# A hybrid decoder layer on one core: conv rows in place, 26 taps in the two-way filter, high parts ahead of low parts, two rows kept for the layer norm

## The chip, the cores and the metric

The kernel runs on one core of a Trainium2 chip. Its time is the device time of one execution in microseconds (us). Three runs of the kernel before took 827.59, 824.11 and 824.79 us, median 824.79 us. A profile is one execution recorded by the hardware profiler. The engines are PE (matmul), PEld (its weight load), DVE (vector), ACT (activation), POOL (GpSimd) and SP (it issues DMAs). POOL issues DMAs too, among them those that add to what lies at their destination.

## What is computed

One layer of a decoder with two mixers, on 1024 prompt positions and 8 sample positions, 1032 columns in all, in fp32:

```python
h = _rmsnorm(x, norm_g)
z = h @ w_in                                        # 1024 -> 6144
a_val, a_gl, a_gate, b_u, b_v, b_gate = split(z)    # 1024 each
a_in = a_val * sigmoid(a_gl)
a_conv = depthwise_conv(concat(conv_buf, a_in), conv_w) + conv_b   # 31 taps
a_out = silu(layernorm(a_conv, a_ln_g, a_ln_b)) * silu(a_gate)
vn = layernorm(b_v, b_ln_g, b_ln_b)
b_out = b_u * spatial_gate(vn, w_s, b_s) * silu(b_gate)
y = x + concat(a_out, b_out) @ w_out                # 2048 -> 1024
y = _rmsnorm(y, final_g)
```

The conv states and the last chunk of `b_v` are outputs as well. The layer norm of the conv branch runs over the 1024 channels, which lie on the partitions of eight tiles, the "rows" k = 0 to 7: its sums over channels are matmuls with a matrix of ones, and they need all eight rows.

## The kernel before

**In-projection.** There are 24 units of two output tiles each: P0 to P7 (values and gates for conv row k), v, B and G (the gMLP's values, its gated part, and the gates of the conv branch). Each step multiplies one unit by both halves of the columns with a seven-product scheme in the manner of Strassen (`PRODS`); the seven products are its "slots". Each fp32 operand is split into a high and a low part, and three passes (high by high, high by low, low by high) make one product, so that a slot has 48 matmuls into PSUM banks za, zb, zc and ze. The weights R of a unit are loaded by SP, summed on DVE (`wsum`, L153), their high parts H made on ACT (`whigh`, L164) and their low parts L on DVE (`wlow`, L168), which needs H. ACT moves partial products between banks (L973, L977, L981); `evac0` (L312, ACT) and `evac1` (L316, DVE) bring results out of PSUM into `row` and `apad`.

**Conv.** For each P unit, 31 taps run over the 1024 prompt positions of row k. Most go through a two-way filter: `d` holds differences of neighbours (L363), and for each pair of taps three DVE operations of 512 elements (L379) add to three tiles m[0], m[1] and m[2], of which the sums m[0]+m[1] and m[0]+m[2] are the even and the odd positions. The taps that are left are products on ACT (`prod`, L389 and L391), added up by POOL's accumulating DMAs (L395). `fin` writes c(k) from m with a step of two elements (L414) and adds the products to it, by a POOL DMA (for k = 7 by DVE). `acc_item` adds c(k) to `ssum` and writes it to DRAM (cD), both by POOL DMAs.

**Layer norm.** The mean's matmuls are lnm and lnms (L437, L440). Each c(k), reloaded from cD as `lc` except for k = 7, is centred (L454, `cen`) and squared on ACT. The squares are summed on DVE, and rows 0 to 3 go back to DRAM. lnv (L480) gives the variance, lnb (L503) spreads its inverse root to `lnr`. Then for each k: DVE multiplies by `lnr` (L523), ACT applies silu, DVE multiplies by the gate (L529), and `prep_m` makes the high part mh on ACT (L695) and the low part ml on DVE (L696). That chain of eight rows is called the chain below.

**Out-projection.** Its first half (steps s = 0 to 7, tiles pz and pzc, 72 matmuls a step) needs only the gMLP branch; its second half (po, three groups of columns by eight tiles) needs the conv branch. pz alternates between banks a and b, pzc is in bank c, and the first po tile goes to bank b, which pz7 held. `evac_h` (L718, L721) and `evac_o` (L726 to L732) add them to yt. After each group `stat_o`, `bcast_o` and `norm_o` make the last rms norm.

**What sets the order.** All large SBUF tiles share one pool of 51 places (tag "u", `NU`): a new tile takes the place that came free, and waits until the engines and DMAs that used it are done. Conv and layer norm work stands in a queue `fill`; `pump` takes from it whenever the estimated DVE time `est["dve"]` is behind the estimated PE time. The costs beside each entry are those estimates. An entry of kind "pe" is taken only from slot 3 on, and behind `delay`s. A larger estimate for DVE moves later entries to later slots.

Of the kernel before, what the change touches and what calls it, by code (L numbers as in the profile page):

```python
# [12 lines left out]
ALU = mybir.AluOpType  # L13
# [12 lines left out]
CW = 31  # L26
H = CW - 1
EPS = 1e-6
NF = 12
NU = 51  # L30
MMT = 0.12
KEEP_C = (4, 5, 6, 7)
KEEP_G = (6, 7)


# [7 lines left out]
def body(ctx, tc, xT, w_in, w_out, state, stateT, conv_w, vecs, wsT, w00, b_s,  # L43
# [7 lines left out]
    def U(shape, name, dt=F32):  # L51
        return pool.tile(shape, dt, tag="u", name=name, bufs=NU)
# [118 lines left out]
    def wsplit(u, i):  # L171
        whigh(u, i)
        wlow(u, i)
# [46 lines left out]
    def warm(n):  # L220
        p = PS("e", f"warm{slotno[0]}_{n}")
        for _ in range(n):
            T.matmul(p[:, 0, :128], lhsT=ones_m, rhs=ident, start=True, stop=True)
# [108 lines left out]
    cc = {}  # L332
    lnc = {}

    def acc_item(k):
        def acc():
            c = cc.pop(k)
            if k == 7:
                V.tensor_tensor(out=Ssum[0], in0=Ssum[0], in1=c, op=ALU.add)
                lnc[7] = c  # L340
                return
            if k == 0:
                Ssum[0] = U([128, NT], "ssum")
                G.dma_start(Ssum[0], c)
            else:
                G.dma_start(Ssum[0], c, accum_op=ALU.add)
            G.dma_start(cD[k], c)
        fill.append(("dve", 1.15 if k == 7 else 0.0, acc))

    def conv_items(k, ap):  # L350

        st = {}
        HN = NP_ // 2
        others = [0] + list(range(2 * NF + 1, CW))

        def start():
            d = U([128, 2, HN + NF - 1], f"d{k}")
            st["d"] = d  # L360
            n = 2 * (HN + NF - 1)
            for e in range(2):
                V.tensor_tensor(out=d[:, e, :], in0=ap[:, 1 + 2 * e:1 + 2 * e + n:2], in1=ap[:, 2:2 + n:2],  # L363
                                op=ALU.subtract)
            mm_ = U([128, 2, HN], f"m01_{k}")
            st["m"] = [mm_[:, 0, :], mm_[:, 1, :], U([128, HN], f"m2_{k}")]
            for e in range(3):
                A.activation(st["m"][e], src(e, 0), AF.Copy, scale=wt(e, 0))
        fill.append(("dve", 1.25, start))

        def src(e, i):
            return ap[:, 2 + 2 * i:2 + 2 * i + NP_:2] if e == 0 else st["d"][:, e - 1, i:i + HN]

        def wt(e, i):
            return cws[:, k, i:i + 1] if e == 0 else cw[:, k, 2 * i + e:2 * i + e + 1]

        def taps(i, e):
            def f():
                V.scalar_tensor_tensor(out=st["m"][e], in0=src(e, i), scalar=wt(e, i), in1=st["m"][e],  # L379
                                       op0=ALU.mult, op1=ALU.add)  # L380
            return f

        def gtap(n):

            def f():
                j = others[n]
                p = U([128, NP_], f"prod{k}_{j}")
                if n == 0:
                    A.activation(p, ap[:, j:j + NP_], AF.Identity, scale=cw[:, k, j:j + 1], bias=vec[:, CB, k:k + 1])  # L389
                else:  # L390
                    A.activation(p, ap[:, j:j + NP_], AF.Copy, scale=cw[:, k, j:j + 1])  # L391
                if n == 0:
                    st["g"] = p
                else:
                    G.dma_start(st["g"], p, accum_op=ALU.add)  # L395
            return f
        n = 0
        for i in range(1, NF):
            while n < len(others) and n * (NF - 3) < i * len(others):
                fill.append(("dve", 0.0, gtap(n)))  # L400
                n += 1
            for e in range(3):
                fill.append(("dve", 0.665, taps(i, e)))
            if i == 4 and k:
                acc_item(k - 1)

        def fin():
            c = U([128, NT], f"c{k}")
            cc[k] = c
            m = st.pop("m")  # L410
            V.scalar_tensor_tensor(out=c[:, NP_:], in0=ap[:, H + NP_:H + NT], scalar=cw[:, k, H:CW],
                                   in1=csmp[:, k, :], op0=ALU.mult, op1=ALU.add)
            for e in range(2):
                V.tensor_tensor(out=c[:, e:NP_:2], in0=m[0], in1=m[1 + e], op=ALU.add)  # L414
            g = st.pop("g")
            if k < 7:
                G.dma_start(c[:, :NP_], g, accum_op=ALU.add)
            else:
                V.tensor_tensor(out=c[:, :NP_], in0=c[:, :NP_], in1=g, op=ALU.add)
        fill.append(("dve", 1.4 if k < 7 else 2.6, fin))  # L420


    ln = {}
    mixa = {}

    def ln_items():
        acc_item(7)

        def lnload(k):
            lnc[k] = U([128, NT], f"lc{k}")  # L430
            SP.dma_start(lnc[k], cD[k])

        def mean():
            ln["m"] = U([128, NT], "lnmean")
            p = PS("e", "lnm")
            for q in range(2):
                T.matmul(p[:, q, :], lhsT=ones_m, rhs=Ssum[0][:, 512 * q:512 * q + 512], start=True, stop=True)  # L437
            A.activation(ln["m"][:, :NP_].rearrange("p (a b) -> p a b", a=2), p, AF.Copy)
            p = PS("e", "lnms")
            T.matmul(p[:, 0, :NS], lhsT=ones_m, rhs=Ssum[0][:, NP_:], start=True, stop=True)  # L440
            A.activation(ln["m"][:, NP_:], p[:, 0, :NS], AF.Copy)
            ln["q"] = U([128, NT], "lnq")
            lnload(0)
            lnload(1)
            dve(2.0)
        fill.append(("delay", 3.0, None))
        fill.append(("pe", 2.0, mean))
# [1 line left out]
        def cen(k):  # L449
            def f():  # L450
                c = lnc[k]
                if k < 5:
                    lnload(k + 2)
                V.tensor_tensor(out=c, in0=c, in1=ln["m"], op=ALU.subtract)  # L454
                if k == 0:
                    A.activation(ln["q"], c, AF.Square)
                else:
                    ln["s", k] = U([128, NT], f"lns{k}")
                    A.activation(ln["s", k], c, AF.Square)
                if k in KEEP_C:  # L460
                    mixa[k] = c
                else:
                    later(lambda: SP.dma_start(ccD[k], lnc.pop(k)), 2)
            return f

        def qacc(k):
            def f():
                V.tensor_tensor(out=ln["q"], in0=ln["q"], in1=ln.pop(("s", k)), op=ALU.add)
            return f
        for k in range(8):  # L470
            fill.append(("dve", 1.15, cen(k)))
            if k >= 2:
                fill.append(("dve", 1.15, qacc(k - 1)))
        fill.append(("dve", 1.15, qacc(7)))

        def var():
            p = PS("e", "lnv")
# [14 lines left out]
        for k in range(8):  # L492
            fill.append(("dve", 1.15, lambda k=k: mixa_norm(k)))
            if k:
                fill.append(("dve", 1.15, lambda k=k - 1: mixa_gate(k)))
        fill.append(("dve", 1.15, lambda: mixa_gate(7)))

    def ln_bc():

# [26 lines left out]
            mixa_load(k + 3)  # L526

    def mixa_gate(k):
        V.tensor_tensor(out=mixa[k], in0=mixa[k], in1=ln.pop(("g", k)), op=ALU.mult)  # L529
        prep_m(0, k)  # L530


# [282 lines left out]
    with tc.manual_schedule():  # L815
# [26 lines left out]
            wsum(u, "S1")  # L842
            wsplit(u, 1)
        bcast_x(0, PS("e", "xbc0"))
        warm(24)
        scale_x(0, 0)
        scale_x(0, 1)
        xpre(0, "nB11")
# [72 lines left out]
        for si, lanes in enumerate(steps):  # L921
# [9 lines left out]
            for slot in range(7):  # L931
# [3 lines left out]
                if si < 2:  # L935
                    start_x(si, slot)

                if si and own and slot == 1:
                    wsplit(u, 3)
                if si and own and slot == 2:  # L940
                    wsplit(u, 4)
                if nxt is not None:
                    if slot == 1:
                        wload(nxt, 2)
                    if slot == (1 if own else 4):
                        wsum(nxt, "S1")
                        wsum(nxt, "S3")
                    if slot == (2 if own else 4):
                        wsum(nxt, "S2")
                    if slot == 4:  # L950
                        wsplit(nxt, 1)
                    elif slot == 5:
                        wsum(nxt, "S4")
                    elif slot == 6:
                        wsplit(nxt, 2)
                if slot == 6:
                    n2 = 2 if si == 0 else u + 2 if own else 3
                    if n2 < N_U:
# [119 lines left out]
        for g in range(NG):  # L1078
            for nt in range(8):
                s = 8 + nt  # L1080
                if nt % 2 == 0:
                    pt[g] = PS(tags[(nt // 2 + 1) % 4], f"po{g}_{nt}")
                po[g, nt] = pt[g][:, nt % 2, :GWS[g]]
                mmo(po[g, nt], s, g, range(0, 2))
                if g == 0 and nt == 0:
# [18 lines left out]
                if g > 0 and 3 <= nt < 6:  # L1104
                    norm_o(g - 1, range(3 * nt - 9, min(3 * nt - 6, 8)))
                mmo(po[g, nt], s, g, range(5, 8))
                if nt % 2:
                    pend = [(g, nt - 1), (g, nt)]
        for x in pend:
            evac_o(*x)  # L1110
        stat_o(2, "b")
        bcast_o(2, "c")
        norm_o(2, range(8))


# [42 lines left out]
```

## Time and profile before

| | |
|---|---|
| runs, median (lowest to highest) | 824.79 us (824.11 to 827.59) |
| profiled execution: its own time | 822.72 us |
| its span in the trace | 821.0 us |
| PE busy | 752.5 us, 92% of the span |
| DVE busy | 606.0 us, 74% |
| ACT busy | 370.6 us, 45% |
| POOL busy | 72.6 us, 9% |

The rows shown below have these forms. A group row gives line, engine, operation, output<-inputs, shapes and count, then busy us and mean ns of one, then the engine's idle time just before these instructions with what released most of it. A row of PE's waits gives the waiting and the releasing instruction, the total in us, the count and the longest. A timeline row gives start and length in us, the instruction, and in brackets the idle time before it with its releaser. A row of windows gives the stretch, its length, the busy time of PE, PEld, DVE, ACT and POOL with instruction counts, then the clock that PE was granted (1.00 is full), the share of the DMA engines and GB/s. A DMA row gives the count, the size and the median us from issue to landing.

### The profile page before, as it was taken

Reading aid. Unit: us, or ns where it says so; the run is one execution under the profiler, and the core shown is the slowest. Engines: PE = TensorE matmul, PEld = TensorE weight load, DVE = VectorE, ACT = ScalarE, POOL = GpSimd, SP = SyncE. Lnnn points to the kernel's source line nnn. Section 1 sums busy time; section 2 is a strip of 40 time slices with the busy share of each in tenths; the row PEclk is TensorE's granted clock in tenths of the full one; section 3 lists DMA queues with packets and bytes.
Section 4 is the critical chain, followed back from the end, with each engine's and each line's share of the span. In section 5 each row is a group of like instructions: output and inputs, shape, how many; then the busy total and the mean of one; then the engine's idle time right before and its main releaser. Section 6 shows DMA issues by size and latency. Waiting matters only on the chain. (4 is left out here: it accounts for less than half of the span.)

```text
span 821.0 us, 13810 instructions
## 1 busy us (share of the span) xinstructions
PE 752.5 (92%) x5648; PEld 738.4 (90%) x5648; DVE 606.0 (74%) x871; ACT 370.6 (45%) x510; POOL 72.6 (9%) x91
## 2 busy tenths in 40 slices
PE   7989999999868999998999997998969997999995
PEld 6989989998868999998999887997859997999994
DVE  4987888887865999997988986887568377343433
ACT  4744545553436575555565644453354244021110
POOL 1100011010011011011020010011000100000000
PEclk8999999999989999999999998998989999999998
DMA  8406256575456569467487476368959422300202
GB/s 317 90 28 210 68 139 165 153 187 163 103 133 193 135 155 235 108 160 198 123 200 186 115 188 155 103 162 191 333 217 374 171 74 78 129 1 0 77 30 101
DMA packets 55031, 122.07 MB, mean 149 GB/s; under 512 B 6232, under 2 KB 21272, under 8 KB 54952
## 3 DMA queue, kind: packets, MB, share of 16 engines
q1 hardware_dynamic: 44600, 83.37, 29.5%
q0 software_dynamic: 10368, 37.82, 23.2%
q8 instruction: 44, 0.72, 0.4%
q14 instruction: 19, 0.16, 0.1%
HBM read 63.63 MB, written 24.38 MB: 107 GB/s over the span
## 5 line engine op out<-in xcount | busy, mean ns | idle before, releaser
L379 DVE SCALAR_TENSOR_TENSOR m<-d,cw,m 128x512 f32<-128x512 f32 x176 | 128.3, 752 | 0.0
L168 DVE TENSOR_TENSOR L<-R,H 128x1024 fp32r<-128x1024 f32 x72 | 87.7, 1220 | 54.0 <-ACT H L164 36.1
L282 PE MATMUL zb<-hT,H 128*128 128x258 f32 x384 | 81.2, 294 | 9.6 <-ACT zb L973 8.8
L282 PE MATMUL zb<-hnB,HL 128*128 128x258 f32 x384 | 71.3, 300 | 17.1 <-DVE row L316 12.2
L164 ACT ACTIVATE H<-R 128x1024 fp32r<-128x1024 f32 x72 | 74.9, 1051 | 25.3 <-DMA prod<-prod 7.2
L282 PE MATMUL zb<-lT,H 128*128 128x258 f32 x384 | 79.0, 288 | 0.0
L282 PE MATMUL zb<-hT,L 128*128 128x258 f32 x384 | 78.8, 287 | 0.0
L282 PE MATMUL za<-hnB,H 128*128 128x258 f32 x384 | 77.9, 285 | 0.0
L282 PE MATMUL za<-lnB,H 128*128 128x258 f32 x384 | 77.6, 284 | 0.0
L282 PE MATMUL za<-hnB,L 128*128 128x258 f32 x384 | 77.3, 283 | 0.0
L282 PEld LDWEIGHTS zb<-hnB,HL 128*128 128x128 f32 x384 | 58.6, 204 | 19.2 <-DVE row L316 13.2
L391 ACT ACTIVATE prod<-apad,cw 128x1024 f32<-128x1024 f32 x48 | 54.8, 1145 | 39.9 <-DMA prod<-prod 24.7
L395 POOL DMA_DIRECT2D prod<-prod x48 | 41.5, 865 | 338.8 <-ACT prod L391 166.3
L282 PEld LDWEIGHTS zb<-hT,H 128*128 128x128 f32 x384 | 60.9, 194 | 11.5 <-ACT zb L973 10.0
L379 DVE SCALAR_TENSOR_TENSOR m<-apad,cws,m 128x512 f32<-128x512 f32 x88 | 65.4, 744 | 0.0
L704 PE MATMUL po<-mh,wl 128*128 128x384 f32 (+1 forms) x192 | 61.6, 321 | 1.2 <-DVE wl L682 1.2
L704 PE MATMUL po<-mh,wh 128*128 128x384 f32 (+1 forms) x192 | 61.7, 321 | 0.0
L704 PE MATMUL po<-ml,wh 128*128 128x384 f32 (+1 forms) x192 | 61.4, 320 | 0.0
L282 PEld LDWEIGHTS zb<-lT,H 128*128 128x128 f32 x384 | 61.0, 194 | 0.0
L282 PEld LDWEIGHTS zb<-hT,L 128*128 128x128 f32 x384 | 60.8, 194 | 0.0
L282 PEld LDWEIGHTS za<-hnB,H 128*128 128x128 f32 x384 | 59.8, 191 | 0.0
L282 PEld LDWEIGHTS za<-lnB,H 128*128 128x128 f32 x384 | 59.8, 191 | 0.0
(185 smaller groups left out, 1748.9 us busy)
## 6 DMA issues: line engine op xcount, KB each, us to landing
R<-w_in SPq DMA_DIRECT2D x96, 256.0 KB, 4.3
prod<-prod POOLq DMA_DIRECT2D x48, 512.0 KB, 5.4
wr<-w_out SPq DMA_DIRECT2D x16, 512.0 KB, 4.7
x<-xT SPq DMA_DIRECT2D x8, 516.0 KB, 6.0
mbD<-row SPq DMA_DIRECT2D x8, 516.0 KB, 5.7
mr<-mbD SPq DMA_DIRECT2D x8, 516.0 KB, 11.3
yt<-xT SPq DMA_DIRECT2D x8, 516.0 KB, 5.1
vD<-va SPq DMA_DIRECT2D x8, 512.0 KB, 4.9
```

What stands on the lines that cost most here:

```text
L164: A.activation(h, R[u, i][:, 0:1, :] if i == 4 else R[u, i], AF.Copy)
L168: V.tensor_tensor(out=l, in0=R[u, i][:, 0:1, :] if i == 4 else R[u, i], in1=h, op=ALU.subtract)
L282: T.matmul(z[:, s, :PW], lhsT=HL[u, wi][we][:, wh, cs], rhs=F[name, p][xe][:, kt, :], start=first, stop=(kt == 3 and we == 1), skip_group_ ...
L379: V.scalar_tensor_tensor(out=st["m"][e], in0=src(e, i), scalar=wt(e, i), in1=st["m"][e], op0=ALU.mult, op1=ALU.add)
L391: A.activation(p, ap[:, j:j + NP_], AF.Copy, scale=cw[:, k, j:j + 1])
L395: G.dma_start(st["g"], p, accum_op=ALU.add)
L704: T.matmul(z, lhsT=w[:, cs], rhs=m_[half, kt][e][:, GS[g]], start=(kt == 0 and e == 0 and w is wh[s]), stop=(kt == KT - 1 and w is wl[s]), ...
```

## The change

The parts, in the order of the diff:

- `NF` goes from 12 to 13: each row has one more pair of taps in the two-way filter and five `prod`s in place of seven.
- Rows 6 and 7 (`RAW_C`) stay on chip for the layer norm. Row 6 is no longer written to cD and read again, and the layer norm goes through the rows as 7, 6, 0, 1, ..., 5. The loads of rows 0 and 1 are issued when row 7 is added.
- m[1] and m[2] live in the two halves of c(k) itself, which therefore holds all even positions and then all odd ones. The products are written in that order (read with a step of two), `fin` adds in place without a step, and the gate puts the positions back into their order: it reads with a step of 512 elements and has an operation of its own for the eight sample columns.
- `acc_item` of the row before enters the queue one pair of taps earlier, and the gate's estimate is 1.25 in place of 1.15.
- 10 warm-up matmuls in place of 24.
- The high parts are made one product ahead of the low parts, which had followed in the same slot.
- In the last group of the out-projection the last tile has PSUM bank b to itself, and the tile before it is evacuated while its matmuls run; the last sums move to banks c and e.

```diff
-NF = 12
+NF = 13
 KEEP_C = (4, 5, 6, 7)
+RAW_C = (6, 7)

     def acc_item(k):
         def acc():
             c = cc.pop(k)
+            if k in RAW_C:
+                lnc[k] = c
             if k == 7:
                 V.tensor_tensor(out=Ssum[0], in0=Ssum[0], in1=c, op=ALU.add)
-                lnc[7] = c
+                lnload(0)
+                lnload(1)
                 return
...
-            G.dma_start(cD[k], c)
+            if k not in RAW_C:
+                G.dma_start(cD[k], c)
...
-            mm_ = U([128, 2, HN], f"m01_{k}")
-            st["m"] = [mm_[:, 0, :], mm_[:, 1, :], U([128, HN], f"m2_{k}")]
+            c = U([128, NT], f"c{k}")
+            st["c"] = c
+            st["m"] = [U([128, HN], f"m{k}"), c[:, :HN], c[:, HN:NP_]]
...
+                pv = p.rearrange("q (e m) -> q e m", e=2)
+                av = ap[:, j:j + NP_].rearrange("q (m e) -> q e m", e=2)
...
-                    A.activation(p, ap[:, j:j + NP_], AF.Copy, scale=cw[:, k, j:j + 1])
+                    A.activation(pv, av, AF.Copy, scale=cw[:, k, j:j + 1])
...
-            if i == 4 and k:
+            if i == 3 and k:
                 acc_item(k - 1)
...
-                V.tensor_tensor(out=c[:, e:NP_:2], in0=m[0], in1=m[1 + e], op=ALU.add)
+                V.tensor_tensor(out=m[1 + e], in0=m[0], in1=m[1 + e], op=ALU.add)
...
+        order = (7, 6, 0, 1, 2, 3, 4, 5)
...
     def mixa_gate(k):
-        V.tensor_tensor(out=mixa[k], in0=mixa[k], in1=ln.pop(("g", k)), op=ALU.mult)
+        a, g = mixa.pop(k), ln.pop(("g", k))
+        gv = g[:, :NP_].rearrange("q (m e) -> q m e", e=2)
+        V.tensor_tensor(out=gv, in0=a[:, :NP_].rearrange("q (e m) -> q m e", e=2), in1=gv, op=ALU.mult)
+        V.tensor_tensor(out=g[:, NP_:], in0=a[:, NP_:], in1=g[:, NP_:], op=ALU.mult)
+        mixa[k] = g
         prep_m(0, k)
...
-        warm(24)
+        warm(10)
...
-                if si and own and slot == 1:
-                    wsplit(u, 3)
-                if si and own and slot == 2:
-                    wsplit(u, 4)
+                if own and slot == 1:
+                    whigh(u, 3)
+                if own and slot == 2:
+                    whigh(u, 4)
+                    wlow(u, 3)
+                if own and slot == 3:
+                    wlow(u, 4)
...
+                    if slot == (3 if own else 4):
+                        whigh(nxt, 1)
                     if slot == 4:
-                        wsplit(nxt, 1)
+                        wlow(nxt, 1)
                     elif slot == 5:
+                        whigh(nxt, 2)
                         wsum(nxt, "S4")
                     elif slot == 6:
-                        wsplit(nxt, 2)
+                        wlow(nxt, 2)
...
-                if nt % 2 == 0:
-                    pt[g] = PS(tags[(nt // 2 + 1) % 4], f"po{g}_{nt}")
+                last = g == 2 and nt == 7
+                if nt % 2 == 0 or last:
+                    pt[g] = PS("b" if last else tags[(nt // 2 + 1) % 4], f"po{g}_{nt}")
...
-                if nt % 2:
+                if last or g == 2 and nt == 6:
+                    pend = [(g, nt)]
+                elif nt % 2:
                     pend = [(g, nt - 1), (g, nt)]
...
-        stat_o(2, "b")
-        bcast_o(2, "c")
+        stat_o(2, "c")
+        bcast_o(2, "e")
```

Three places of the engines' programs follow. In rows of the changed kernel the line numbers are its own: L165 is the high part, L715 the out-projection's matmul, L530 the multiplication by `lnr`, L538 and L539 the gate, L707 the low part ml, L729 and L732 `evac_h`. Numbers in names tell tiles apart.

The first place is ACT in one unit of the in-projection, before. H_3, HL_4 and H_1 are high parts; row_15 is the evacuation after the fourth product.

```order
L164 ACTIVATE H_3_4228<-R_3_3915 128x1024
L977 ACTIVATE p_15_4260<-ze_4227 128x516
L601 ACTIVATE vh_3979<-vh_3979,rs 128x128 x4
L164 ACTIVATE HL_4_4268<-R_4_3913 128x512
L981 ACTIVATE zc_4296<-zb_4223 128x2x258
L312 ACT_TABLE_LOAD
L312 ACTIVATE row_15_4327<-za_4195 128x2x258
L164 ACTIVATE H_1_4341<-R_1_4159 128x1024
```

And the same stretch of ACT in the changed kernel:

```order
L165 ACTIVATE H_3_4173<-R_3_3856 128x1024
L994 ACTIVATE p_15_4204<-ze_4172 128x516
L612 ACTIVATE vh_3920<-vh_3920,rs 128x128 x4
L165 ACTIVATE HL_4_4213<-R_4_3854 128x512
L998 ACTIVATE zc_4241<-zb_4165 128x2x258
L165 ACTIVATE H_1_4247<-R_1_4102 128x1024
L313 ACT_TABLE_LOAD
L313 ACTIVATE row_15_4275<-za_4137 128x2x258
```

H_1, the high part for the next unit, has moved ahead of the evacuation; the low parts of the third and fourth weights stand a slot later on DVE than before.

The second place is PE where the mean of the layer norm is taken. Before, it stands in the last unit, 62 rows of PE ahead of the first pz:

```order
L282 MATMUL zb_6252<-hT_1_624,L_3_6266 128x258
L437 MATMUL lnm<-ssum,ones_m 128x512 x2
L440 MATMUL lnms<-ssum,ones_m 128x8
L282 MATMUL zb_6252<-hT_0_338,H_3_6265 128x258
L282 MATMUL zb_6252<-hT_1_624,H_3_6265 128x258
```

In the changed kernel it stands in step s = 2 of the out-projection, behind 156 matmuls of pz and pzc:

```order
L715 MATMUL pz_6608<-mh_6401,wl_6535 128x384
L446 MATMUL lnm<-ssum,ones_m 128x512 x2
L449 MATMUL lnms<-ssum,ones_m 128x8
L715 MATMUL pz_6608<-mh_6373,wh_6533 128x384
L715 MATMUL pz_6608<-ml_6374,wh_6533 128x384
```

The variance moves with it from behind 192 of the 576 matmuls of the first half to behind 336, and lnb from behind 228 to behind 372. Fourteen of row 7's tap operations, its sum and its addition to `ssum` stand behind the first pz as well.

The third place is DVE at the end of the chain, before (yt_6810, yt_6950 and yt_7050 belong to pz5, pz6 and pz7; ml_7143 is the last low part):

```order
L529 TENSOR_TENSOR c_6259<-c_6259,row_23_6422 128x1032
L696 TENSOR_TENSOR ml_7143<-c_6259,mh_7142 128x1032
L718 TENSOR_TENSOR yt_6810<-pz_7047,yt_6810 128x768
L721 TENSOR_TENSOR yt_6712<-pzc_6947,yt_6712 128x264
L721 TENSOR_TENSOR yt_6810<-pzc_6947,yt_6810 128x264
L682 TENSOR_TENSOR wl_7167<-wr_7048,wh_7165 128x1024
L718 TENSOR_TENSOR yt_6950<-pz_7146,yt_6950 128x768
L682 TENSOR_TENSOR wl_7247<-wr_7148,wh_7245 128x1024
L718 TENSOR_TENSOR yt_7050<-pz_7229,yt_7050 128x768
```

And in the changed kernel, where yt_6928 belongs to pz7 and ml_7205 is the last low part:

```order
L530 TENSOR_TENSOR c_5346<-c_5346,lnr 128x1032
L538 TENSOR_TENSOR sg_7003<-lc_6762,sg_7003 128x1024
L539 TENSOR_TENSOR sg_7003<-lc_6762,sg_7003 128x8
L707 TENSOR_TENSOR ml_7191<-sg_7003,mh_7190 128x1032
L530 TENSOR_TENSOR c_6012<-c_6012,lnr 128x1032
L538 TENSOR_TENSOR row_23_6296<-c_5346,row_23_6296 128x1024
L539 TENSOR_TENSOR row_23_6296<-c_5346,row_23_6296 128x8
L707 TENSOR_TENSOR ml_7199<-row_23_6296,mh_7198 128x1032
L538 TENSOR_TENSOR row_23_6335<-c_6012,row_23_6335 128x1024
L539 TENSOR_TENSOR row_23_6335<-c_6012,row_23_6335 128x8
L707 TENSOR_TENSOR ml_7205<-row_23_6335,mh_7204 128x1032
L729 TENSOR_TENSOR yt_6928<-pz_7166,yt_6928 128x768
```

Before, the evacuation of pz7 stands behind those of pz5 and pz6 and two weight splits that follow the chain; now it follows on the chain's last low part.

More of the change, by code (lines that the diff above doesn't have):

```diff
@@ L333, in body, with lnload @@
     lnc = {}
+    def lnload(k):
+        lnc[k] = U([128, NT], f"lc{k}")
+        SP.dma_start(lnc[k], cD[k])
     def acc_item(k):
@@ L387, in f @@
                 p = U([128, NP_], f"prod{k}_{j}")
+                pv = p.rearrange("q (e m) -> q e m", e=2)
+                av = ap[:, j:j + NP_].rearrange("q (m e) -> q e m", e=2)
                 if n == 0:
-                    A.activation(p, ap[:, j:j + NP_], AF.Identity, scale=cw[:, k, j:j + 1], bias=vec[:, CB, k:k + 1])
+                    A.activation(pv, av, AF.Identity, scale=cw[:, k, j:j + 1], bias=vec[:, CB, k:k + 1])
                 else:
-                    A.activation(p, ap[:, j:j + NP_], AF.Copy, scale=cw[:, k, j:j + 1])
+                    A.activation(pv, av, AF.Copy, scale=cw[:, k, j:j + 1])
                 if n == 0:
@@ L403, in conv_items @@
                 fill.append(("dve", 0.665, taps(i, e)))
-            if i == 4 and k:
+            if i == 3 and k:
                 acc_item(k - 1)
         def fin():
-            c = U([128, NT], f"c{k}")
-            cc[k] = c
+            c = cc[k] = st.pop("c")
             m = st.pop("m")
@@ L426, in ln_items @@
     def ln_items():
+        order = (7, 6, 0, 1, 2, 3, 4, 5)
         acc_item(7)
-        def lnload(k):
-            lnc[k] = U([128, NT], f"lc{k}")
-            SP.dma_start(lnc[k], cD[k])
         def mean():
@@ L442, in mean @@
             ln["q"] = U([128, NT], "lnq")
-            lnload(0)
-            lnload(1)
             dve(2.0)
@@ L451, in f @@
                 c = lnc[k]
-                if k < 5:
+                if k < 4:
                     lnload(k + 2)
                 V.tensor_tensor(out=c, in0=c, in1=ln["m"], op=ALU.subtract)
-                if k == 0:
+                if k == order[0]:
                     A.activation(ln["q"], c, AF.Square)
@@ L469, in qacc @@
             return f
-        for k in range(8):
+        for n, k in enumerate(order):
             fill.append(("dve", 1.15, cen(k)))
-            if k >= 2:
-                fill.append(("dve", 1.15, qacc(k - 1)))
-        fill.append(("dve", 1.15, qacc(7)))
+            if n >= 2:
+                fill.append(("dve", 1.15, qacc(order[n - 1])))
+        fill.append(("dve", 1.15, qacc(order[7])))
         def var():
@@ L494, in ln_items @@
             if k:
-                fill.append(("dve", 1.15, lambda k=k - 1: mixa_gate(k)))
-        fill.append(("dve", 1.15, lambda: mixa_gate(7)))
+                fill.append(("dve", 1.25, lambda k=k - 1: mixa_gate(k)))
+        fill.append(("dve", 1.25, lambda: mixa_gate(7)))
     def ln_bc():
```

## The prediction

> **What bounds the kernel now.** I read the page's busy times first, then the waits of PE between 112 and 606 us (the in-projection once its order has settled), then the timeline around the long waits, then the windows there for the granted clock.
>
> ```profile
> PE 752.5 (92%) x5648; PEld 738.4 (90%) x5648; DVE 606.0 (74%) x871; ACT 370.6 (45%) x510; POOL 72.6 (9%) x91
> ...
> L379 DVE SCALAR_TENSOR_TENSOR m<-d,cw,m 128x512 f32<-128x512 f32 x176 | 128.3, 752 | 0.0
> L168 DVE TENSOR_TENSOR L<-R,H 128x1024 fp32r<-128x1024 f32 x72 | 87.7, 1220 | 54.0 <-ACT H L164 36.1
> ...
> L391 ACT ACTIVATE prod<-apad,cw 128x1024 f32<-128x1024 f32 x48 | 54.8, 1145 | 39.9 <-DMA prod<-prod 24.7
> ```
>
> PE is busy 92% of the span, and the change removes no matmul. It can win only PE's idle time and time in which PE runs at a lower clock. Two idle columns name candidates: DVE's low parts (L168) wait 36.1 us for ACT's high parts, and ACT's products (L391) wait 24.7 us for POOL's accumulating DMAs.
>
> ```profile
> PE zb L282 <- DVE row L316: 12.2, 5, 5.0
> PE zb L282 <- ACT zb L973: 7.9, 3, 5.6
> PE vps L553 <- ACT va L546: 6.8, 1, 6.8
> PE zb L282 <- DVE apad L316: 4.8, 3, 2.4
> PE gs L624 <- DVE t L615: 2.3, 2, 1.2
> ```
>
> These are PE's own waits there: total, number, longest. They add up to 34.0 us. The releaser is a PSUM evacuation, but the timeline shows what had held it:
>
> ```profile
> 236.54 1.22 DVE L168 TENSOR_TENSOR L<-R,H 128x1024 fp32r<-128x1024 f32 x1 [6.57 <-DMA prod<-prod]
> ...
> 240.06 0.59 PE L553 MATMUL vps<-ident,row 128*8 128x128 f32 x2 [6.82 <-ACT va L546]
> ...
> 504.31 1.15 ACT L391 ACTIVATE prod<-apad,cw 128x1024 f32<-128x1024 f32 x1 [7.15 <-DMA prod<-prod]
> ...
> 506.62 0.80 PE L282 MATMUL zb<-hT,H 128*128 128x258 f32 x2 [5.58 <-ACT zb L973]
> ...
> 566.00 1.23 DVE L168 TENSOR_TENSOR L<-R,H 128x1024 fp32r<-128x1024 f32 x1 [3.25 <-DMA prod<-prod]
> ...
> 567.88 0.80 PE L282 MATMUL zb<-hnB,HL 128*128 128x258 f32 x2 [3.87 <-DVE row L316]
> ...
> 597.58 1.23 DVE L454 TENSOR_TENSOR lc<-lc,lnmean 128x1032 f32<-128x1032 f32 x1 [8.27 <-DMA lc<-cD]
> ...
> 599.47 0.80 PE L282 MATMUL zb<-hnB,HL 128*128 128x258 f32 x2 [5.05 <-DVE row L316]
> ```
>
> Four times DVE or ACT stands still for a DMA with the evacuation queued behind it, and PE then waits 6.82, 5.58, 3.87 and 5.05 us. In the first three the DMA accumulates a product: its source tile is one of the 51 shared tiles, and a new tile takes its place. In the fourth it is the reload of a conv row for the layer norm. The windows behind such gaps show a second price:
>
> ```profile
> 240.10:244.10 4.00, 4.00 (x23) 3.92 (x24) 4.00 (x12) 0.90 (x2) 0.00 (x0) 0.64 0.42 132
> 506.70:512.70 6.00, 6.00 (x28) 6.00 (x29) 6.00 (x10) 3.83 (x8) 0.01 (x1) 0.50 0.70 178
> 568.00:574.00 6.00, 6.00 (x28) 6.00 (x29) 5.01 (x8) 2.68 (x4) 0.87 (x1) 0.50 0.58 111
> 599.50:605.50 6.00, 6.00 (x28) 6.00 (x29) 2.98 (x3) 3.56 (x6) 0.00 (x0) 0.56 0.42 170
> ```
>
> The third number from the end is the granted clock. Length times what is missing of 1.00 is lost: 1.4, 3.0, 3.0 and 2.6 us.
>
> **In-projection.** NF 13 moves two of seven products for each row from ACT to DVE: 24 more L379 at 0.752, 18.0 us of DVE; 16 fewer ACT products at 1.145, 18.3 us of ACT; 16 fewer of these DMAs:
>
> ```profile
> prod<-prod POOLq DMA_DIRECT2D x48, 512.0 KB, 5.4
> ...
> cD<-c POOLq DMA_DIRECT2D x7, 516.0 KB, 8.8
> ```
>
> The queue then has 32 of 48 accumulations, more widely spread. The split high parts start a product before the low parts that need them, which answers the 36.1 us. One tile fewer is held by each conv row, but its c lives from the row's start until the sum and the 8.8 us write have read it.
>
> What I count:
> - The wait at 599.47 goes with its cause, since rows 7 and 6 need no load and rows 0 and 1 are requested long before use: −5.1, and −2.6 of clock.
> - Of the 34.0 us, 28.9 are left, and 7.4 of clock: 36.3. Three waits are traced to product DMAs: 6.82 + 5.58 + 3.87 = 16.3, with 1.4 + 3.0 + 3.0 of clock, 23.7. A third of those DMAs goes and the rest spread, but DVE gets fuller, so I let two thirds go: −15.8. Of the other 12.6 the lead of the high parts covers only what waits for ACT; I let a third go: −4.2. Together **−20.0**, bounds 0 and −36.3.
> - The strided product reads on ACT lie under ACT's 45% and are costed at nothing; without that cover a doubling would be 40 times 1.145, 46 us of ACT, still under PE.
> - Fewer warm-up matmuls: 0. The first matmuls on real data wait for ACT's evacuation, not for the warm-up:
>
> ```profile
> 33.88 0.51 PE L282 MATMUL zb<-hT,H 128*128 128x258 f32 x2 [0.95 <-ACT zb L973]
> ```
>
> If the clock rises later for it, the loss is another half-clock stretch, 3.0.
>
> **From the first half of the out-projection to its second.** Before, the mean's matmuls stand inside the last unit; after, in step 2. Everything of the layer norm from the mean to lnb stands two steps later, and the second half's first product (po) now waits for the evacuation of pz7, which stands behind the last low part on DVE.
>
> ```profile
> 586.61 1.88 PE L437 MATMUL lnm<-ssum,ones_m 128*128 128x512 f32 x4
> ...
> 589.61 0.39 PE L440 MATMUL lnms<-ssum,ones_m 128*128 128x8 f32 x2 [1.11 <-ACT lnmean L438]
> ...
> 604.80 0.36 PE L704 MATMUL pz<-mh,wh 128*128 128x384 f32 x1
> ...
> 620.97 0.34 PE L704 MATMUL pz<-mh,wh 128*128 128x384 f32 x1
> ...
> 632.24 0.34 PE L704 MATMUL pz<-mh,wh 128*128 128x384 f32 x1
> ...
> 647.72 1.95 PE L503 MATMUL lnb<-ident,rs 128*128 128x128 f32 x16
> ...
> 651.53 1.23 DVE L523 TENSOR_TENSOR ma<-ma,lnr 128x1032 f32<-128x1032 f32 x1 [6.63 <-ACT lnr L508]
> ...
> 694.41 1.23 DVE L696 TENSOR_TENSOR ml<-c,mh 128x1032 fp32r<-128x1032 f32 x1 [1.19 <-ACT mh L695]
> ...
> 713.01 0.35 PE L704 MATMUL po<-mh,wh 128*128 128x384 f32 x1
> ```
>
> The mean's 1.88 + 1.11 + 0.39 = 3.4 us leave the in-projection (−3.4) and come back here. Step 0 takes 16.2 us (604.80 to 620.97), a clean step 11.3. Of the excess 4.9, I let 3.0 go, as step 0 starts behind the stalled layer norm. Call the first pz P. Before, lnb starts at P+42.9. After: 42.9 − 3.0 + two steps 22.5 + 3.4 = P+65.8. The chain starts 3.8 later (647.72 to 651.53), at P+69.6. It takes 44.1 to the end of the last low part (695.64), and then:
> - the gate's extra 128x8 operation, eight times at about 0.17 (what DVE takes for the variance's 128x8 below): 1.4
> - the evacuation of pz7, as before about 0.9
>
> ```profile
> 642.69 0.17 DVE L482 TENSOR_SCALAR rs<-lnv 128x8 f32<-128x8 f32 x1 [8.28 <-PE lnv L480]
> ```
>
> So po starts at P+116.0. PE itself has 204 of 576 matmuls left at lnb, 2.83 steps, and is done at P+69.6+31.9 = P+101.5: it idles 14.5 us, and pays a half-clock stretch of 3.0 behind it. P+119.0 against 713.01 − 604.80 = P+108.2: **+10.8**. The mean's own sum, which waits for row 7's last taps, is on POOL and DVE early in this stage and I count no wait for it.
>
> The gate now reads one operand with a step of 2048 bytes. The trace has no such row. The nearest has a step of 8 bytes:
>
> ```profile
> L414 DVE TENSOR_TENSOR c<-m,m 128x512 f32<-128x512 f32 x8 | 5.5, 684 | 0.0
> ```
>
> Its 684 ns for 512 elements are no more than the matching share of L696's 1.23 us for 1032, so I take 0. The other end, a doubling as I set it, is eight times 1.23, 9.8 us, all on the chain and before po. In the Trainium skill, "SBUF — State Buffer", section "Specifications (TRN2)", has lines of 16 bytes that must be hit at least twice for full bandwidth, with a penalty for each new line. By that rule the 8-byte step is free, as the row shows, and the 2048-byte step is not; this trace cannot show its price.
>
> **End.**
>
> ```profile
> 808.22 0.43 DVE L726 TENSOR_TENSOR yt<-po,yt 128x264 f32<-128x264 f32 x1 [3.08 <-PE po L704]
> ...
> 809.20 0.43 DVE L732 TENSOR_TENSOR osq<-osq 128x264 f32<-128x264 f32 x1 [0.55 <-ACT osq L730]
> ...
> 810.54 1.00 PE L742 MATMUL ov<-ones_m,osq 128*128 128x1 f32 x10 [0.47 <-ACT osq L730]
> ```
>
> Two tiles are evacuated one after the other behind the last matmul. With one of them done during the last product, ov starts where the first square ends, at about 809.2: −1.3.
>
> **Sum**, on the profiled execution, 822.7: −3.4 −7.7 −20.0 +10.8 −1.3 = −21.6, 801.1. The runs' median 824.8 is 2.1 above that execution, so **803.2**.
>
> **Rivals.**
> - All in-projection waits go: 16.3 more, **786.9**. For it: every long one has a DMA or a high part as its cause. Against: DVE was busy 402.37 of 494 us there, and 18.0 more in a stage that is 30 us shorter would be 91%:
>
> ```profile
> 112.00:606.00 494.00, 457.64 (x3656) 449.88 (x3655) 402.37 (x596) 253.89 (x361) 56.91 (x68) 0.97 0.65 169
> ```
>
> - The waits stay, and the change does not do what it says: 32 DMAs of 5.4 us still sit before the same tiles. Then −1.6 is all: **823.2**. Against: a third of the cause is gone.
> - The gate pays the doubled price: 9.8 more idle before po: **813.0**. For: the rule above; against: no row.
> - Slower: the place of c(k). Tiles are handed on as DMAs finish, c is held longer, and the order shows ACT's and DVE's first tiles of later units waiting for the write of c(k) to DRAM, at 8.8 us. If each of the seven handovers stalls as the one before 506.62 did, each costs 5.58 + 3.0 = 8.6, 60.2 instead of 36.3: 20.0 + 23.9 = 43.9 more than forecast, **847.1**. It turns slower from the fifth such wait: 36.3 + 1.6 + 4.1 = 42.0, and five times 8.6 are 43.0. Against: two of eight rows no longer write at all. For: the trace has one such wait already, an evacuation into apad that waited 2.6 us for a write of c:
>
> ```profile
> L316 DVE TENSOR_TENSOR apad<-zb,p 128x516 f32<-128x516 f32 x6 | 4.1, 689 | 2.7 <-DMA cD<-c 2.6
> ```
>
> **How the numbers follow.** Chances: forecast 0.48, gate 0.16, all go 0.16, waits stay 0.11, slower 0.09. About 0.5%, 4.1 us, is what a measurement of this kernel can tell from no change. The range reaches from 786 to 823: the better end of the in-projection's bounds to the case in which none goes; it leaves out the slower case and a little at each end. Faster 0.81 (the first three and a little of the fourth), same 0.10, slower 0.09.
>
> **What would show it.** Right: L391 and its POOL DMA x32; L168's wait for ACT H far below 36.1; no wait like the one at 599.47; the mean's matmuls in step 2; a PE wait of some 14 us before the first po, released by DVE yt; the gate's strided operation at about 1.2 us; ov one evacuation after the last matmul. Wrong: PE waits of over 3 us with DMA cD or prod behind them; a gate near 2.4 us; or step 2 waiting for the mean.

## The result and the profile after

The changed kernel takes 794.68 us in the median of four runs (791.79 to 796.09), against 824.91 us: a ratio of 0.9624, 95% interval 0.9589 to 0.9658. The forecast was 803.2 us with a range of 786 to 823. The profiled execution is the fastest of the four, 791.79 us with a span of 790.1 us.

The page of the changed kernel first, the rows that answer to those of before:

```profile
PE 737.3 (93%) x5620; PEld 726.5 (92%) x5620; DVE 621.3 (79%) x903; ACT 358.4 (45%) x494; POOL 57.9 (7%) x74
...
L169 DVE TENSOR_TENSOR L<-R,H 128x1024 fp32r<-128x1024 f32 x72 | 87.6, 1220 | 1.9 <-ACT H L165 1.6
...
L408 POOL DMA_DIRECT2D prod<-prod x32 | 27.8, 868 | 357.2 <-ACT prod L404 316.2
```

DVE's low parts wait 1.6 us for ACT, where it had been 36.1. Next PE's waits between 111 and 564 us, up to its first pz:

```profile
PE zb L283 <- DVE row L317: 7.2, 1, 7.2
PE zb L283 <- ACT zb L990: 1.8, 1, 1.8
PE rsum L811 <- POOL wst L806: 1.4, 1, 1.4
PE zb L283 <- DVE L L169: 1.3, 1, 1.3
```

Without rsum, which stands ahead of the conv work, 10.3 us are left. Before it was 36.1 us: the 34.0 of the prediction's five rows, and three smaller ones of 2.1 us, 1.1 of which belong to the mean. The windows over the same stage and behind the two longest waits:

```profile
100.00:564.00 464.00, 452.22 (x3731) 448.76 (x3730) 411.65 (x612) 244.59 (x351) 45.15 (x54) 0.99 0.58 158
...
559.20:565.20 6.00, 6.00 (x31) 5.96 (x31) 2.74 (x4) 3.43 (x5) 0.00 (x0) 0.64 1.04 326
680.50:686.50 6.00, 5.97 (x19) 6.00 (x20) 2.83 (x4) 0.00 (x0) 0.00 (x0) 0.51 0.00 0
```

The granted clock is 0.99 in place of 0.97. Summed over windows of 4 us from rsum to the first pz, what is missing of full clock falls from 15.3 to 3.4 us. The timeline of the one long wait that is left, and of the out-projection:

```profile
554.41 1.06 ACT L691 ACTIVATE wh<-wr 128x1024 fp32r<-128x1024 f32 x1 [7.54 <-DMA prod<-prod]
...
559.19 0.80 PE L283 MATMUL zb<-hnB,HL 128*128 128x258 f32 x2 [7.19 <-DVE row L317]
...
564.09 0.34 PE L715 MATMUL pz<-mh,wh 128*128 128x384 f32 x1
...
595.93 0.39 PE L449 MATMUL lnms<-ssum,ones_m 128*128 128x8 f32 x2 [1.11 <-ACT lnmean L447]
...
632.28 1.95 PE L510 MATMUL lnb<-ident,rs 128*128 128x128 f32 x16
...
680.53 0.66 PE L715 MATMUL po<-mh,wh 128*128 128x384 f32 x1 [12.45 <-DVE yt L729]
...
779.53 1.00 PE L753 MATMUL ov<-ones_m,osq 128*128 128x1 f32 x10 [0.93 <-ACT osq L741]
```

| stretch | before | after | difference |
|---|---|---|---|
| start to the first pz | 604.80 | 564.09 | −40.7 |
| first pz to first po | 108.2 | 116.4 | +8.2 |
| first po to the last ov | 97.5 | 99.0 | +1.5 |
| last ov to the end | 10.5 | 10.6 | +0.1 |
| span | 821.0 | 790.1 | −30.9 |

The in-projection gave 40.7 us, and the out-projection took 9.8 of them back.

### The profile page after: what moved, and what is told of

It reads as the page before. It is cut to its first block, busy times and chain, and to the rows that moved or that the text cites. A ratio compares the mean times of both kernels' runs of the same rounds, so it can differ in the third digit from the quotient of the medians.

```text
span 790.1 us, 13716 instructions
## 1 busy us (share of the span) xinstructions
PE 737.3 (93%) x5620; PEld 726.5 (92%) x5620; DVE 621.3 (79%) x903; ACT 358.4 (45%) x494; POOL 57.9 (7%) x74
## 5 line engine op out<-in xcount | busy, mean ns | idle before, releaser
L390 DVE SCALAR_TENSOR_TENSOR c<-d,cw,c 128x512 f32<-128x512 f32 x192 | 139.4, 747 | 0.0
L165 ACT ACTIVATE H<-R 128x1024 fp32r<-128x1024 f32 x72 | 75.7, 1055 | 12.9 <-DVE R L154 7.0
L283 PE MATMUL zb<-hT,H 128*128 128x258 f32 x384 | 78.9, 287 | 1.8 <-ACT zb L990 1.8
L283 PE MATMUL zb<-lT,H 128*128 128x258 f32 x384 | 77.3, 283 | 0.0
L715 PE MATMUL po<-mh,wh 128*128 128x384 f32 (+1 forms) x192 | 62.9, 328 | 12.5 <-DVE yt L729 12.5
L283 PE MATMUL zb<-hnB,HL 128*128 128x258 f32 x384 | 67.5, 288 | 7.2 <-DVE row L317 7.2
L390 DVE SCALAR_TENSOR_TENSOR m<-apad,cws,m 128x512 f32<-128x512 f32 x96 | 71.7, 747 | 0.0
L715 PE MATMUL po<-mh,wl 128*128 128x384 f32 (+1 forms) x192 | 62.7, 326 | 1.2 <-DVE wl L693 1.2
L283 PEld LDWEIGHTS zb<-hnB,HL 128*128 128x128 f32 x384 | 55.7, 194 | 7.7 <-DVE row L317 7.4
L715 PE MATMUL po<-ml,wh 128*128 128x384 f32 (+1 forms) x192 | 62.4, 325 | 0.0
L283 PEld LDWEIGHTS zb<-hT,H 128*128 128x128 f32 x384 | 59.3, 189 | 2.5 <-ACT zb L990 2.1
L283 PEld LDWEIGHTS zb<-lT,H 128*128 128x128 f32 x384 | 59.4, 189 | 0.0
L283 PEld LDWEIGHTS za<-hnB,L 128*128 128x128 f32 x384 | 59.3, 189 | 0.0
L408 POOL DMA_DIRECT2D prod<-prod x32 | 27.8, 868 | 357.2 <-ACT prod L404 316.2
```

Of the source, the lines that this page charges most:

```text
L165: A.activation(h, R[u, i][:, 0:1, :] if i == 4 else R[u, i], AF.Copy)
L283: T.matmul(z[:, s, :PW], lhsT=HL[u, wi][we][:, wh, cs], rhs=F[name, p][xe][:, kt, :], start=first, stop=(kt == 3 and we == 1), skip_group_ ...
L715: T.matmul(z, lhsT=w[:, cs], rhs=m_[half, kt][e][:, GS[g]], start=(kt == 0 and e == 0 and w is wh[s]), stop=(kt == KT - 1 and w is wl[s]), ...
```

## Experiments

Theory A is that the accumulating DMAs of the conv's products carried the in-projection's waits: their tiles come free late, and what waits for the place is an instruction of ACT or DVE with a PSUM evacuation behind it. Theory B gives the gain to the high parts' lead over the low parts. The first four runs each undo one part of the changed kernel.

**24 taps** (`e1`).

```diff
-NF = 13
+NF = 12
```

> The changed kernel with the two-way filter back at 24 taps (7 products for each row). Theory A (the accumulating DMAs of the products carry most of the in-projection's waits): with 48 of these DMAs instead of 32, PE's waits between 100 us and the first pz, 14.4 us in the changed kernel, grow to 25 us or more, and the time by 10 to 20 us. Theory B (the high parts made a product ahead took the waits away): the waits stay below 18 us and the time moves by less than 4 us either way.

806.39 us (806.13 to 808.21), 11.7 above the changed kernel; ratio to before 0.9762 (0.9695 to 0.9828). From the group rows, the waits and the timeline of this run:

```profile
L169 DVE TENSOR_TENSOR L<-R,H 128x1024 fp32r<-128x1024 f32 x72 | 87.6, 1219 | 34.9 <-ACT H L165 14.3 <-DMA prod<-prod 11.1 <-DMA cD<-c 9.5
```

```profile
PE zb L283 <- ACT zc L998: 8.1, 4, 3.1
PE vps L564 <- ACT va L557: 5.4, 1, 5.4
PE lnms L449 <- ACT lnmean L447: 3.4, 1, 3.4
```

```profile
580.73 0.39 PE L449 MATMUL lnms<-ssum,ones_m 128*128 128x8 f32 x2 [3.41 <-ACT lnmean L447]
...
589.75 0.34 PE L715 MATMUL pz<-mh,wh 128*128 128x384 f32 x1
...
696.67 0.34 PE L715 MATMUL po<-mh,wh 128*128 128x384 f32 x1
```

The DMAs are back as releasers, PE's waits in the stage (all rows but rsum's) add up to 26.8 us, and the first pz comes 25.7 us later. But the mean stands in the last unit again, and po starts 106.9 us behind the first pz in place of 116.4, without a long wait. The times are those that theory A expected, and it is `NF` that moves the layer norm: 24 more entries of 0.665 in the estimate of DVE push it back. That order, and DVE's share, go back with the DMAs here, so that this run alone does not show the DMAs as the cause; `e5` and `e6` take the two apart.

The run shows one thing more. The kernel before took 825.86 us in the same series, so the parts other than `NF` bring 19.5 us at 24 taps. Which of them does it was not taken apart.

**The lead undone** (`e2`).

```diff
-                    whigh(u, 3)
+                    wsplit(u, 3)
...
-                        whigh(nxt, 1)
...
-                        wlow(nxt, 1)
+                        wsplit(nxt, 1)
```

> The changed kernel with the high parts back in the same slot as the low parts. Theory B: DVE's low parts wait for ACT's high parts again (1.6 us in the changed kernel, 36.1 before), PE's waits in the in-projection grow by 10 us or more and the time by 10 to 20 us. Theory A: DVE waits some 20 to 36 us for the high parts, but PE's own waits grow by less than 6 us, since DVE has room for them.

794.04 us (792.19 to 794.79): no difference. Its group row and its waits from 114 to 563 us:

```profile
L169 DVE TENSOR_TENSOR L<-R,H 128x1024 fp32r<-128x1024 f32 x72 | 87.7, 1220 | 32.9 <-ACT H L165 31.5 <-DMA c<-prod 1.2
```

```profile
PE zb L283 <- ACT zb L984: 3.4, 1, 3.4
PE zb L283 <- DVE row L317: 2.6, 2, 1.5
```

DVE waits 31.5 us again, and PE does not wait more. With 26 taps theory B falls: DVE had the room. The wait of 7.19 us in the last unit is not there in this run (the longest is 1.1), although its loads are those of the changed kernel; of the 3.5 us that the stage is shorter, the way from the first pz to the first po, 119.2 us, loses 2.8 again.

**Rows in tiles of their own** (`e3`) and **row 6 reloaded, order 0 to 7** (`e4`).

```diff
-            st["m"] = [U([128, HN], f"m{k}"), c[:, :HN], c[:, HN:NP_]]
+            mm_ = U([128, 2, HN], f"m01_{k}")
+            st["m"] = [mm_[:, 0, :], mm_[:, 1, :], U([128, HN], f"m2_{k}")]
...
-        V.tensor_tensor(out=gv, in0=a[:, :NP_].rearrange("q (e m) -> q m e", e=2), in1=gv, op=ALU.mult)
+        V.tensor_tensor(out=a, in0=a, in1=g, op=ALU.mult)
```

> The changed kernel with the conv rows built beside c in tiles of their own as before (one tile more for each row, products and c in natural order, no strided gate). If the spared tile carried the gain: PE's waits in the in-projection grow by 5 to 15 us. If it did not: in-projection within 3 us, and the chain behind lnb 1 to 2 us shorter, since the gate's extra operation of 0.15 us is gone eight times.

```diff
-RAW_C = (6, 7)
+RAW_C = (7,)
...
-        order = (7, 6, 0, 1, 2, 3, 4, 5)
+        order = (0, 1, 2, 3, 4, 5, 6, 7)
```

> The changed kernel with row 6 written and reloaded again, the layer norm in the order 0 to 7, and the loads of rows 0 and 1 issued with the mean, as before. Forecast's reason (the wait of 5.05 us in the last unit came from the reload): the mean stands in step 2 of the out-projection in this kernel too, so the stall of DVE for the reload, 8.27 us before, falls into that step; the first pz stays within 2 us, and the first po comes 3 to 9 us later. Rival: the reload is hidden behind work in that step and the time moves by less than 2 us.

791.18 us (789.48 to 793.51) and 791.52 us (790.33 to 793.73). Neither part brings a gain; both medians lie 3 us below the changed kernel's, whose own runs spread over 4.3 us, so that I do not call them faster. In `e3` the in-projection is within 0.2 us of the changed kernel's, and from lnb to the first po it is 1.0 us shorter, as expected without the gate's second operation; the spared tile carries no gain. In `e4` the first po starts 117.3 us behind the first pz, against 116.4: the reload is hidden, as the rival said.

**ACT's time or the DMAs?** (`e5`, `e6`) Two products with scale 0 for each row bring back the work of 24 taps on ACT, with and without their DMAs, while the filter keeps 26; the output stays what it is. The products are spread over as many pairs of taps as with 24 (`NF - 4`).

```diff
-        others = [0] + list(range(2 * NF + 1, CW))
+        others = [0] + list(range(2 * NF - 1, CW))
...
-                    A.activation(pv, av, AF.Copy, scale=cw[:, k, j:j + 1])
+                    A.activation(pv, av, AF.Copy, scale=0.0 if j <= 2 * NF else cw[:, k, j:j + 1])
...
-                else:
+                elif j > 2 * NF:          # e6 only
                     G.dma_start(st["g"], p, accum_op=ALU.add)
...
-            while n < len(others) and n * (NF - 3) < i * len(others):
+            while n < len(others) and n * (NF - 4) < i * len(others):
```

> The changed kernel (26 taps in the filter) with two more products for each row whose scale is 0 and which are accumulated like the others: ACT, POOL and the DMAs do the work of 24 taps, DVE that of 26. Theory A (the accumulating DMAs carry the waits): PE's waits between 100 us and the first pz grow from 11.7 us to 22 us or more, and the time by 10 us or more. Rival (24 taps were slower for another reason, the order or DVE's share): the waits stay below 16 us and the time within 4 us.

> As the run before, but the two products of scale 0 are made and not accumulated: ACT's 16 products and their tiles are there, the 16 DMAs are not. Theory A: as the changed kernel, within 4 us, waits below 16 us. Rival (ACT's time carries the waits): as the run with the DMAs, 10 us or more slower.

814.00 us (811.60 to 814.66) with the DMAs, 795.62 us (794.98 to 796.35) without: 16 DMAs of 512 KB cost 18.4 us, and 16 products on ACT 0.9 us, which is within the spread of the changed kernel's runs. The size is as theory A said and the place is not: before the first pz, PE's waits without rsum's are 13.5 us, where 22 or more were expected, and the largest follows in step 0, as the timeline of `e5` shows:

```profile
577.89 0.87 POOL L408 DMA_DIRECT2D prod<-prod  x1 [9.25 <-DMA prod<-prod]
588.09 2.02 ACT L706 ACTIVATE mh<-mr 128x1032 fp32r<-128x1032 f32 x2 [11.65 <-issue]
588.66 0.86 POOL L408 DMA_DIRECT2D prod<-prod  x1 [9.90 <-DMA prod<-prod]
589.21 0.69 PE L715 MATMUL pz<-mh,wh 128*128 128x384 f32 x1 [11.79 <-ACT mh L706]
```

Row 7's accumulations follow one another, each waiting over 9 us for the one before. What held mh its row does not name, but SP's waits from 560 to 595 us do:

```profile
SPq L698 <- DMA prod<-prod: 16.8, 2, 8.9
```

L698 is the load of mr, mh's input. It stands in SP's queue for the place of a product, goes out at 577.3 us and takes 10.9 us to land, until 588.2; mh starts at 588.09.

`e1` and `e5` make the same 48 accumulations and the same products on ACT, and differ in the 24 operations of DVE and the order that follows from them. Stage by stage, in us (waits of PE before the first pz without rsum's; lost clock summed over windows of 4 us):

| | rsum to first pz | PE's waits there | lost clock there | first pz to first po |
|---|---|---|---|---|
| before | 493.0 | 36.1 | 15.3 | 108.2 |
| `e1`, 24 taps | 477.0 | 26.8 | 5.1 | 106.9 |
| `e5`, 26 taps, 48 DMAs | 459.0 | 13.5 | 3.4 | 130.5 |
| `e6`, 26 taps, 32 DMAs | 450.9 | 8.0 | 1.6 | 118.7 |
| changed kernel | 452.4 | 10.3 | 3.4 | 116.4 |

From `e1` to `e5` the in-projection gets 18 us shorter with no DMA less: the mean and other entries move behind the first pz, and waits go or move with them. Behind the first pz over 23 us come back. From `e5` to `e6` both stages get shorter, by 8.1 and 11.7 us. So the medians split the 11.7 us between `e1` and the changed kernel: 7.6 lost by DVE's longer work and its order, 18.4 gained by fewer DMAs, 0.9 by less of ACT. (The kernel before took 825.86 us in the series of `e1` and 826.46 in that of `e5` and `e6`.)

**26 taps alone** (`e7`): the kernel before with `NF = 13`.

> The kernel before with 26 taps in the filter and nothing else. Theory A: this part alone takes most of the in-projection's waits, which fall from 37 us to 20 us or less, and the mean moves to step 2; 800 us or less. Rival (the change needs its other parts, the tile that is spared above all): the longer DVE work meets the same tiles, and the time stays above 810 us.

794.35 us (793.78 to 795.08), ratio 0.9612 (0.9597 to 0.9626): one number gives all of the change's gain. The gains of the parts do not add: the others bring 19.5 us with 24 taps (`e1`), and nothing beside 26. PE's waits before the first pz, without rsum's, fall to 7.1 us. Its low parts still wait for ACT, row 6 is reloaded, no tile is spared:

```profile
L168 DVE TENSOR_TENSOR L<-R,H 128x1024 fp32r<-128x1024 f32 x72 | 87.7, 1221 | 32.0 <-ACT H L164 31.8
```

The mean stands at 596.37 and the first po waits 13.11 us here too.

**The wait before po** (`e8`, `e10`). In the chain DVE stands still for 1.18 us in each row, until ACT has made the high part; `e8` issues the next row's work in between. `e10` also gives the first po bank e, which nothing holds.

```diff
-        prep_m(0, k)
+        lows.append(prep_m(0, k, False))
+        if len(lows) > 1 or k == 7:
+            lows.popleft()()
+        if k == 7:
+            lows.popleft()()
```

> The changed kernel with each low part of the chain behind lnb put off until the next row's multiplication and gate are issued, so that DVE no longer stands still for ACT's high part (1.18 us a row). If the 12.45 us for which PE waits before the first po come from the length of this chain: the chain gets 8 to 9 us shorter, the wait falls to about 4 us, and the time by 8 to 11 us. Rival (PE waits for something beside the chain, the banks or the weights): less than 3 us.

```diff
-                    pt[g] = PS("b" if last else tags[(nt // 2 + 1) % 4], f"po{g}_{nt}")
+                    pt[g] = PS("b" if last else "ecba"[nt // 2] if g == 0 else tags[(nt // 2 + 1) % 4],
+                               f"po{g}_{nt}")
```

> As the run with the low parts put off, and the first po tile in a bank of its own, so that it no longer waits for the evacuation of pz7 behind the chain. Chain theory: of the 4.98 us that PE still waits there, the matmuls of six of the eight rows (3.2 us) now run within, and a wait of 1 to 2 us for the last low part is left; 2 to 5 us faster than that run with the half-clock stretch behind it. Rival (the wait is the last low part's anyway): within 1 us of that run.

784.08 us (783.48 to 785.74) and 780.86 us (780.32 to 782.60). PE's waits, first of `e8`, then of `e10`:

```profile
673.18 0.66 PE L726 MATMUL po<-mh,wh 128*128 128x384 f32 x1 [4.98 <-DVE yt L740]
```

```profile
676.03 0.44 PE L726 MATMUL po<-mh,wl 128*128 128x384 f32 x1 [1.71 <-DVE wl L699]
```

The wait was the chain's length, and then the bank. What is left of it is hardly the last low part (0.21 us) but a weight's low part, which stands behind the chain on DVE.

**One tile fewer** (`e9`: `NU = 50`).

> The changed kernel with 50 shared tiles in place of 51. If what matters is how long tiles are held by accumulating DMAs, not how many there are: one tile less costs less than 4 us. Rival (the pool is at its limit, and fewer products helped by asking for fewer tiles): waits in the in-projection grow by 6 us or more, the time by 6 us or more.

800.69 us (800.12 to 800.88), 6.0 slower: the rival's time, but not its place. PE's waits before the first pz do not grow; most of the loss lies between the first pz and the mean, as the windows of `e9` and of the changed kernel over that stretch show:

```profile
566.63:603.97 37.34, 31.88 (x163) 27.93 (x161) 27.19 (x34) 12.08 (x13) 1.56 (x2) 0.86 0.68 229
```

```profile
564.09:595.93 31.84, 28.03 (x162) 25.05 (x160) 25.95 (x32) 11.09 (x12) 0.86 (x1) 1.00 0.43 147
```

5.5 us more, with a clock of 0.86, which alone is 5.2 us. So in this run the number of tiles counts too, at the pass to the out-projection.

**The wait at 559.19** (`e11`), and **all together** (`e12`: the edits of `e3`, `e8`, `e10` and `e11`).

```diff
-                    if 1 <= slot < 3:
-                        load_w(slot - 1)
-                        load_y(slot - 1)
+                    if slot in (1, 5):
+                        load_w(slot // 4)
+                    if slot in (5, 6):
+                        load_y(slot - 5)
```

> The changed kernel with the loads of the second weight and of the first two residual tiles issued three to four slots later in the last unit. If the 7.19 us wait there comes from full DMA engines (their share is 1.0 from 540 us on), which delay a product's accumulation that ACT's next tile waits for: the wait falls by 2 us or more and the time by 2 to 6 us. Rival (the accumulation is late for a reason of its own): the wait stays at 6 us or more.

> All of these together with the rows in tiles of their own in natural order: the low parts put off, the bank, the later loads. If the gains add up: 8 to 11 us for the chain, 2 to 5 for the bank, 2 to 6 for the loads, about 1.5 for the gate, so 773 to 782 us.

`e11`: 791.18 us (790.45 to 791.51), with this in its timeline:

```profile
556.52 1.23 DVE L707 TENSOR_TENSOR ml<-mr,mh 128x1032 fp32r<-128x1032 f32 x1 [5.18 <-DMA prod<-prod]
...
559.08 0.80 PE L283 MATMUL zb<-hnB,HL 128*128 128x258 f32 x2 [4.82 <-DVE row L317]
```

The wait falls by 2.4 us, and DVE now stands where ACT stood, for the same kind of DMA. The loads are at most a part of its cause: in `e2` and `e6`, which leave them alone, no wait of over 1.1 us is left there. Nor is a gain in time shown: `e3` and `e4`, with the changed kernel's loads, have the same median. `e12`: 777.13 us (776.36 to 778.20), ratio to before 0.9416 (0.9391 to 0.9442), within what was expected and 17.6 us below the changed kernel. The single gains (`e3` 3.5, `e8` 10.6, `e10` another 3.2, `e11` 3.5) would make 20.8; those of `e3` and `e11` lie within the spread of runs.

## Why the prediction came out as it did

- **Direction and range were right, and the mechanism in its main part**: waits that end at product DMAs went, with the half-clock stretches behind them. `e7` shows that 26 taps alone are enough, `e5` and `e6` that fewer accumulations are worth 18.4 us and ACT's time about none. What I did not see is that the longer DVE work moves so much of the order: of the shorter in-projection a part is work and waits that come back behind the first pz. And the parts overlap: without the 26 taps the others still bring 19.5 us (`e1`).
- **The term that was mis-sized is "two thirds of the three DMA waits and a third of the others"**, −20.0. With the −3.4 and −7.7 the forecast had −31.1 for the in-projection; −40.7 was measured. All three DMA waits went, and of the others all but 3.1 us; a new wait of 7.19 came. The 34.0 was itself short by 1.0, since it left out two small rows beside that of the mean. Waits fell by 24.7 (35.0 to 10.3, the mean's apart) where I counted 20.2 (5.1, two thirds of 16.3, and 4.2). Clock came back by 11.9 where I counted 7.5: I had priced three stretches beside the last one, while the whole stage lost 15.3. That is 8.9 of the 9.6 us; for the other 0.7 I have no term. How much of the 9.6 the DMAs gave and how much the order was not taken apart in the kernel before.
- **The reason for the −7.7 is not the one that acts.** I wrote that the wait at 599.47 goes because rows 7 and 6 need no load. In `e4` and `e7` the reload is back and the wait is not: with 26 taps the layer norm leaves the last unit. Only where the mean stays there can the kept rows have a part in it: in `e1` rows 6 and 7 are kept, and the longest wait for an evacuated row is 0.8 us. That was not taken apart.
- **The lead of the high parts was priced as a share of −4.2 and is worth nothing with 26 taps** (`e2`), though it took 34.5 us of waiting from DVE.
- **The pass to po was right, its exact size by luck**: P+116.0 forecast, 116.4 measured; an idle time of 14.5 against 12.45; a half-clock stretch of 3.0, as the window from 680.50 has it (0.49 of 6 us). With it, +11.2 against +10.8. Two errors offset each other. lnb starts at P+68.2, not 65.8: step 0 takes 15.45 us after 16.17 before, so that 0.7 went where I let 3.0 go. And from its start to the end of the last low part the chain takes 43.4 us, not 45.5: before, DVE stood 1.40 us in it for the high part of a weight (at 682.63), which it does not now, and what is left of the difference makes the gate's eight extra operations some 0.7 us, not 1.4. I had put it down to the order as a whole; `e1` and `e7` show that the number of taps does it.
- **The gate's strided read costs next to nothing**, where I chose 0:

```profile
L538 DVE TENSOR_TENSOR sg<-ma,sg 128x1024 f32<-128x1024 f32 x4 | 5.1, 1266 | 0.2 <-ACT ma L531 0.2
...
L538 DVE TENSOR_TENSOR row<-c,row 128x1024 f32<-128x1024 f32 x2 | 2.5, 1232 | 0.0
```

With a step of 2048 bytes it takes 1232 to 1266 ns for 1024 elements, before 1228 for 1032 without a step. The doubling that I had set against the penalty in the Trainium skill's "SBUF — State Buffer", section "Specifications (TRN2)", did not come; the measurement decides. My reading of L414 was wrong, though: its matching share of 1.23 us for 1032 elements is 610 ns, not 684. By a straight line through L718 (768 elements, 0.95 us) and L529 (1032 elements, 1.23 us), both without a step, 512 elements take about 0.68 us, an estimate, so that the step was cheap all the same.
- **The end was right**: behind the first po's half-clock stretch, 99.0 − 3.0 = 96.0 us to the last ov against 97.5 before, −1.5 where I had −1.3. The warm-up was right at 0: rsum starts at 111.71 and 111.84 us.
- **The slower rival did not come** at 26 taps: ACT and DVE wait 3.7 us for writes of c(k) in the changed kernel, and waited 6.0 before. Its mechanism exists: in `e1`, with 24 taps and c(k) held longer, these waits are 24.6 us.

## What to carry to other kernels

Follow a wait of the bounding engine back to what held the engine that released it, and price the whole stage's lost clock with it, not only the long gaps. What an accumulating DMA costs does not show in the busy time of the engine that issues it (POOL, 7 to 9% of the span): it keeps a tile of a full pool until it lands, an instruction or a load waits for that place, and its successors wait for it in a row. The largest idle time in a table (36.1 us of DVE here) may cost nothing, and work that an estimate places elsewhere can take back a quarter of a gain; both show only in the wait that ends last there. Parts of a change can relieve the same wait: take each out alone, and also put it in alone, before one is called the cause.

## What had not been expected of the hardware

The granted clock fell without any long gap. In `e9` five waits of 1.44, 0.83, 0.95, 0.51 and 0.58 us within 9 us, with PE partly waiting between them, brought it to 0.50 from about 572 to 581 us, while in the kernel before a single wait of 2.42 us left it at 1.00. And ACT's products, read with a step of two elements, take 1240 ns in place of 1145; in `e3`, without the step, they take 1144.
